# A fused two-block kernel: a new table of engine times for its side work, and key low parts of both attentions on 128 rows

## The chip, the cores and the metric

One core of one Trainium2 chip. The time is the device time of one execution in microseconds (us), the median of repeated runs; the profile is one execution taken apart. Engines: PE (TensorE, matmuls), ACT (ScalarE), DVE (VectorE), POOL (GpSimd) and SP (SyncE, which only starts transfers). Each engine works through its own queue in order and waits for the others by semaphores.

## The reference, cut to what matters

The input `x` has 512 tokens of 1024 features. The first block is a short convolution branch, a gated delta rule with 8 heads of 128 features in chunks of 64 tokens, and a feed-forward net with a convolution. The second block has a pooling mixer, a top-k attention `dsa` and a forgetting attention `fox` with 6 heads of 64 features each, an output projection and a last norm.

```python
# delta rule, per chunk: a triangular system, then a scan over chunks
L = where(strict, einsum('bnhid,bnhjd->bnhij', k_beta, k) * decay, 0.0)
sol = triangular_solve(eye + L, rhs, left_side=True, lower=True)
def step(state, inp):
    v_new = u_c - einsum('bhcd,bhde->bhce', w_c, state)
    o = einsum('bhcd,bhde->bhce', q_c, state) + einsum('bhij,bhje->bhie', A_c, v_new)
    state = state * exp(gl)[..., None] + einsum('bhcd,bhce->bhde', k_c, v_new)
    return state, o
# forgetting attention, F = cumsum(log f):
s = einsum('bqhd,bkhd->bhqk', q[:, s0:e], k[:, :e]) * sm_scale
s = s + F[:, :, s0:e, None] - F[:, :, None, :e]
# dsa: the same product, masked to the keys that a top-k over indexer scores selects
```

## The kernel before, in words

**The main stream.** All activations stand with features on partitions and the 512 tokens along the row. Every projection is cut into tiles of 128 output features (`tiles`, L304 to L348). `run` (L1544) does one tile: for each 128 input features three matmuls of 512 columns, high weight times high activation, high times low, low times high (L1582 to L1586), because each 32-bit value is split into a rounded high part and a low part. I call these the main matmuls. The class `Weights` (L195) loads a tile's weights (`w_raw`, three buffers) by SP's queue, ACT copies the high part (`w_hi`) and POOL or DVE subtracts to give the low part (`w_lo`).

**The side work.** Everything else is written as generators: `head` (L634) and `subst` (L837) for the delta rule, `attend` (L1352) for attention, `ev_keys` (L1238) and its like for what follows each tile. Every six main matmuls `tick` (L370) resumes the generators, and each emits its next few instructions into the engines' queues. A generator is skipped while what it emitted last isn't finished by a guessed clock: `Clock.add` (L76) holds a table of costs per engine and operation and keeps the time at which each engine and each tile is done. So that table decides behind which main matmul a side instruction stands, and in which order DVE, POOL and ACT do theirs. A guess that is too early makes an engine wait in its queue; one that is too late leaves the result unused.

**The delta rule.** For each pair of heads, `subst(p)` inverts triangular blocks in 30 steps of two instructions, on POOL for p = 0 and 2 and on DVE for p = 1 and 3; its matrix `sub_l` comes from DRAM and goes back to DRAM (`dr`) by SP's queue, and a scratch tile is `sub_t`. `head` computes `k` against `k` and `q` with high and low parts `kqh` and `kql` (the low ones made on POOL), then, with the inverse, scans four groups of 128 tokens (L770 to L789): each link is a matmul, then DVE (`r`, or the state `St`) or ACT (`w`), then the next matmul.

**The attentions.** For each pair of heads `ev_queries` makes `q[i]` with the high part of head i on its own 64 rows and its low part on the other 64. `ev_keys` makes `k[0]` and `k[1]`, the high part of each head on all 128 rows, and one tile `k[2]` with the low parts, head 0 on rows 0 to 63 and head 1 on rows 64 to 127. `attend` takes one head and 128 queries at a time, 48 units in all, 12 for each width of 128, 256, 384 and 512 keys. A unit has two matmuls for the scores: `q[i]` against `k[i]` over 128 rows (L1378), and its own 64 rows against those of `k[2]` (L1379). Then DVE adds the mask and takes the maximum, ACT exponentiates, PE transposes and multiplies by the values.

**Memory.** The second block's slots are 29 tiles `slot_c` of 128x512 in the pool `p3`, beside the tiles `fin` of the output (L1661 to L1664).

In the trace, slots are named by their kind (`slot_f`, `slot_x`, `slot_r`, `slot_t` in the first block, `slot_c` in the second); `GT` and `hsm` hold the delta rule's small factors, `cm` constants, `tiny` small columns. Nearly all instructions have the line L142, that of the helper through which they pass, so groups are told apart by their tiles.

Of the kernel before, what the change touches and what calls it, by code (L numbers as in the profile page):

```python
# [11 lines left out]
OP = mybir.AluOpType  # L12
# [41 lines left out]
class Clock:  # L54
# [4 lines left out]
    def __init__(self):  # L59
        self.t = {k: 0.0 for k in ("pe", "act", "v", "p", "dma")}  # L60
        self.end, self.bus = 0.0, {}
        self.wrote, self.read = {}, {}

    @property
    def pe(self):
# [10 lines left out]
    def add(self, kind, method, args, kw):  # L76
        aps = [(k, v) for k, v in [(None, v) for v in args] + list(kw.items())
               if hasattr(v, "tensor") and hasattr(v, "shape")]
        if "out" in kw:
            out = kw["out"]  # L80
        else:
            out = aps.pop(0)[1]
        outs = [out] + [v for k, v in aps if k == "accum_out"]
        ins = [v for k, v in aps if k not in ("out", "accum_out")]
        n = 1
        for v in (kw["in_"] if method == "max" else out).shape[1:]:
            n *= v
        lag = 100
        if method == "dma":
            c = 525  # L90
        elif kind == "pe":
            if method == "transpose":
                c = 109
            elif kw["rhs"].dtype == R32:
                c = max(0.42 * n, 107)
            else:
                c = max(1.68 * n, 1.68 * kw["lhsT"].shape[-1])
            lag = 250
        elif kind == "act":
            c = 70 + 0.88 * n + (180 if isinstance(kw.get("scale"), bass.AP) else 0)  # L100
        elif kind == "v":
            c = 70 + (0.52 if method in ("tensor_scalar", "tensor_copy", "memset") else 1.04) * n
        elif kind == "p":
            c = 145 + (1.2 if method == "memset" else 2.13) * n
            if kw.get("op") == OP.pow:
                c = 950
        s = self.t[kind]
        if not (kind == "pe" and kw.get("start") is False):
            for v in outs:
                k = self.key(v)  # L110
                s = max(s, self.read.get(k, 0), self.wrote.get(k, 0) if kind != "pe" else 0)
        for v in ins:
            s = max(s, self.wrote.get(self.key(v), 0))
        e = self.t[kind] = s + c
        for v in ins:
            k = self.key(v)
            self.read[k] = max(self.read.get(k, 0), e)
        if method == "dma":
            self.bus[kind] = max(self.bus.get(kind, 0), e) + 4 * out.shape[0] * n / 340
            e = self.bus[kind] + 1800  # L120
        e += lag
        for v in outs:
            self.wrote[self.key(v)] = e
        self.end = max(self.end, e)


class Engine:
# [124 lines left out]
def build(tc, A, out):  # L252
# [29 lines left out]
    def slots(pool, kind, n):  # L282
        return [(pool, f"slot_{kind}{i}") for i in range(n)]
# [118 lines left out]
    def need(n, keep=None):  # L402
        while len(FS.free) < n + (reserve[0] if keep is None else keep):
            yield
# [833 lines left out]
    def ev_keys(ps, n, j):  # L1238

        yield from wait_r2()  # L1240
        yield from need(1)
        t = FS.get()
        vtt(t, ps, rrow, OP.mult)
        MB.put(ps)
        yield
        yield from need(3)
        k = [FR.get() for _ in range(3)]
        for i in range(2):
            for o in (64 * i, 64 - 64 * i):
                act(k[i][o:o + 64], t[64 * i:64 * i + 64])  # L1250
        yield
        for i in range(2):
            rows_ = slice(64 * i, 64 * i + 64)
            PL.tensor_tensor(out=k[2][rows_], in0=t[rows_], in1=k[i][rows_].bitcast(F32), op=OP.subtract)
        FS.put(t)
        B2[n, j] = k
        if n == "dk":
            return
        while "F" not in B2:
            yield  # L1260
        yield from need(2)
# [90 lines left out]
    def attend():  # L1352
        while units:
            u = next_unit()
            if u is None:
                yield
                continue
            units.remove(u)
            m, j, qt, i = u
            w = (qt + 1) * 128  # L1360
            tok = slice(qt * 128, qt * 128 + 128)
            if (m, j) not in done:
                obank[m, j] = SB.get()
                done[m, j] = 0
                spawn(finish(m, j))
            P = FS.get()
            if m == "f":
                mask = FS.get()
                act(mask[:, :w], B2["fF", j][i][:, :w], AF.Identity, bias=B2["F"][:, qt, 2 * j + i:2 * j + i + 1])
                ptt(mask[:, w - 128:w], mask[:, w - 128:w], cmask, OP.add)  # L1370
                yield 1000
                while len(SB.free) < 2:
                    yield
            else:
                mask = B2["sel", qt] if qt else amask[:, 384:]
            b = SB.get()
            q, k, half_ = B2[m + "q", j][i], B2[m + "k", j], slice(64 * i, 64 * i + 64)
            PE.matmul(b[:, :w], lhsT=q[:, tok], rhs=k[i][:, :w], start=True, stop=False)  # L1378
            PE.matmul(b[:, :w], lhsT=q[half_, tok], rhs=k[2][half_, :w], start=False, stop=True)  # L1379
            mx, nm = tcol()[:, 0:1], tcol()[:, 0:1]  # L1380
            V.tensor_tensor_reduce(out=P[:, :w], in0=b[:, :w], in1=mask[:, :w], scale=1.0, scalar=-3e38, op0=OP.add,
                                   op1=OP.max, accum_out=mx)
            SB.put(b)
            if m == "f":
                FS.put(mask)
            V.tensor_scalar(out=nm, in0=mx, scalar1=-1.0, scalar2=None, op0=OP.mult)
            yield
# [226 lines left out]
    for i, (kind, key, ids) in enumerate(tiles):  # L1614
# [29 lines left out]
        if kind == "down" and key == 7:  # L1644
            await_(lambda: len(FS.free) == 12, "second phase")
            for j in range(NF):
                RS.put(*act_[j])
            RS.free = [t for t in RS.free if t in BASE]
            P2.close()
            P3 = ctx.enter_context(ExitStack())  # L1650
            p3 = P3.enter_context(tc.tile_pool(name="p3", bufs=1))
            m2 = p3.tile([128, 2, 512], F32, name="m2")
            amask, cmask = m2[:, 0], m2[:, 1, 384:]
            pw = p3.tile([128, 2, 128], F32, name="pw")
            pinv = p3.tile([128, 2, 17], F32, name="pinv")
            misc = p3.tile([128, 56], F32, name="misc")
            top8 = p3.tile([128, 4, 8], F32, name="top8")
            asum = {m: p3.tile([128, 3, 4, 2], F32, name=f"asum{m}") for m in "fd"}
            arec = {m: p3.tile([128, 3, 4, 2], F32, name=f"arec{m}") for m in "fd"}
            spawn(load_consts())  # L1660
            FS = Slots(slots(p3, "c", 29))  # L1661
            FR = Slots(FS.free, R32)
            last = [[p3.tile([128, n, 256], F32, name=f"fin{s}{g}") for g, n in enumerate((3, 3, 2))]
                    for s in range(2)]  # L1664
            reserve[0] = 4
            for q in (1, 2, 3):
                spawn(scores(q))
            spawn(score_cleanup())
            for _ in range(NATT):
                spawn(attend())  # L1670
        if kind == ORDER2[-1][0] and key == ORDER2[-1][1]:
            for j in range(8):
                RS.put(*h2g[j])
# [89 lines left out]
```

## Time and profile before

| | |
|---|---|
| median of 3 runs | 1352.42 us (1351.46 to 1353.33) |
| the profiled execution: its own time | 1349.59 us |
| its span, first to last instruction | 1347.8 us |
| PE busy | 1296.9 us (96%), 6388 matmuls |
| DVE, POOL, ACT busy | 777.1, 698.7, 591.2 us (58, 52, 44%) |
| share of the chain that ended last | PE 80%, DVE 9%, POOL 3% |
| granted TensorE clock, mean | 0.990 of full |

How to read it: the profiled execution was 2.8 us faster than the median of the runs. Matmuls overlap, so the busy time of one is longer than its share; the distance from one start to the next is what a matmul costs. An idle time in brackets behind an instruction names what released it.

### The profile page before, as it was taken

Reading aid. Unit: us, or ns where it says so; the run is one execution under the profiler, and the core shown is the slowest. Engines: PE = TensorE matmul, PEld = TensorE weight load, DVE = VectorE, ACT = ScalarE, POOL = GpSimd, SP = SyncE. Lnnn points to the kernel's source line nnn. Section 1 sums busy time; section 2 is a strip of 40 time slices with the busy share of each in tenths; the row PEclk is TensorE's granted clock in tenths of the full one; section 3 lists DMA queues with packets and bytes.
Section 4 is the critical chain, followed back from the end, with each engine's and each line's share of the span. In section 5 each row is a group of like instructions: output and inputs, shape, how many; then the busy total and the mean of one; then the engine's idle time right before and its main releaser. Section 6 shows DMA issues by size and latency. Waiting matters only on the chain.

```text
span 1347.8 us, 17771 instructions
## 1 busy us (share of the span) xinstructions
PE 1296.9 (96%) x6388; PEld 1058.8 (79%) x6388; DVE 777.1 (58%) x1331; ACT 591.2 (44%) x1348; POOL 698.7 (52%) x624
## 2 busy tenths in 40 slices
PE   6899999899999999999999999999999899999996
PEld 4688787778877788888888888888888677787785
DVE  5667869775757541324576666652334387677533
ACT  5355454554563343333344444443333366654431
POOL 5777882338624132225554444454665665545466
PEclk9999999999999999999999999999999899999998
DMA  6224323232233223334333333233333422112131
GB/s 221 96 71 136 92 86 122 63 114 75 54 115 89 92 64 109 94 112 139 94 95 101 101 95 94 94 102 91 98 102 104 124 76 78 60 51 63 48 93 64
DMA packets 59252, 127.06 MB, mean 94 GB/s; under 512 B 13454, under 2 KB 28046, under 8 KB 59164
## 3 DMA queue, kind: packets, MB, share of 16 engines
q1 hardware_dynamic: 59164, 125.93, 30.3%
q8 instruction: 50, 0.82, 0.3%
q14 instruction: 38, 0.31, 0.1%
HBM read 117.49 MB, written 6.84 MB: 92 GB/s over the span
## 4 chain that ended last, share of the span: by engine, by line
PE 80%; DVE 9%; POOL 3%; issue 3%; ACT 2%; DMA 2%; SPq 0%; DVEq 0%; POOLq 0%; ACTq 0%
PE bank L142 80%; DVE slot_f L142 2%; DVE slot_r L142 2%; DMA w_raw<-in_w_in 2%; POOL w_lo L142 1%; DVE slot_c L142 1%; DVE sub_t L142 1%; ACT slot_f L142 1%; DVE w_lo L142 1%; POOL slot_f L142 1%; DVE sub_l L142 1%; DVE tiny L142 0%; DVE fin L142 0%; ACT w_hi L142 0%; POOL tiny L142 0%
## 5 line engine op out<-in xcount | busy, mean ns | idle before, releaser
L142 PE MATMUL bank<-slot_r,w_hi 128*128 128x512 f32 (+1 forms) x1924 | 611.4, 395 | 1.3 <-POOL slot_r L142 1.3
L142 POOL TENSOR_TENSOR w_lo<-w_raw,w_hi 128x512 fp32r<-128x512 f32 x240 | 317.6, 1329 | 421.9 <-ACT w_hi L142 386.4
L142 PEld LDWEIGHTS bank<-slot_r,w_hi 128*128 128x128 f32 x1924 | 353.9, 189 | 72.1 <-issue 1.9
L142 PE MATMUL bank<-slot_r,w_lo 128*128 128x512 f32 (+1 forms) x944 | 368.0, 390 | 0.7 <-POOL w_lo L142 0.7
L142 ACT ACTIVATE w_hi<-w_raw 128x512 fp32r<-128x512 f32 (+1 forms) x408 | 249.2, 623 | 117.8 <-PE bank L142 92.6
L142 DVE TENSOR_TENSOR w_lo<-w_raw,w_hi 128x512 fp32r<-128x512 f32 x164 | 146.1, 899 | 128.2 <-ACT w_hi L142 124.3
L142 PEld LDWEIGHTS bank<-slot_r,w_lo 128*128 128x128 f32 x944 | 177.9, 188 | 38.8 <-POOL w_lo L142 1.1
L142 PE MATMUL bank<-slot_f,w_hi 128*128 128x512 f32 x488 | 163.4, 406 | 11.1 <-ACT slot_f L142 8.2
L142 PEld LDWEIGHTS bank<-slot_f,w_hi 128*128 128x128 f32 x488 | 90.5, 191 | 34.1 <-ACT slot_f L142 9.9
L142 PE MATMUL bank<-slot_x,w_hi 128*128 128x512 f32 x340 | 113.8, 400 | 0.0
L142 DVE SCALAR_TENSOR_TENSOR slot_b<-slot_b,pc,slot_b 128x511 f32<-128x511 f32 x88 | 87.1, 989 | 22.1 <-ACT slot_b L142 20.5
L142 PE MATMUL bank<-slot_t,w_hi 128*128 128x512 f32 x272 | 96.8, 397 | 0.0
L142 PE MATMUL bank<-slot_f,w_lo 128*128 128x512 f32 x212 | 84.2, 397 | 0.6 <-POOL w_lo L142 0.6
L142 PE MATMUL bank<-slot_x,w_lo 128*128 128x512 f32 x204 | 80.3, 394 | 0.0
L142 PEld LDWEIGHTS bank<-slot_x,w_hi 128*128 128x128 f32 x340 | 62.6, 190 | 12.3
L142 PE MATMUL bank<-slot_a,w_hi 128*128 128x512 f32 x224 | 69.0, 389 | 0.0
L142 ACT ACTIVATE slot_c<-bank 128x512 f32<-128x512 f32 (+5 forms) x82 | 34.9, 466 | 76.5 <-PE bank L142 76.4
L142 PEld LDWEIGHTS bank<-slot_c,slot_c 128*128 128x128 f32 x336 | 48.3, 190 | 18.3 <-issue 12.6
L142 PE MATMUL bank<-slot_c,slot_c 128*128 128x64 f32 (+4 forms) x336 | 62.6, 305 | 0.0
L142 ACT ACTIVATE slot_r<-bank 128x128 f32<-128x128 f32 (+4 forms) x92 | 31.8, 353 | 68.0 <-PE bank L142 50.2
L142 DVE TENSOR_TENSOR slot_x<-bank,slot_x 128x512 f32<-128x512 f32 (+1 forms) x19 | 12.6, 664 | 82.2 <-PE bank L142 82.2
L142 ACT ACTIVATE slot_f<-bank 128x128 f32<-128x128 f32 (+3 forms) x106 | 33.4, 333 | 60.5 <-PE bank L142 44.0
(279 smaller groups left out, 1882.8 us busy)
## 6 DMA issues: line engine op xcount, KB each, us to landing
w_raw<-in_w_in SPq DMA_DIRECT2D x103, 512.0 KB, 3.6
w_raw<-in_w_up SPq DMA_DIRECT2D x44, 512.0 KB, 3.5
w_raw<-in_w_down SPq DMA_DIRECT2D x16, 512.0 KB, 3.6
w_raw<-in_w_a SPq DMA_DIRECT2D x8, 512.0 KB, 3.5
w_raw<-in_w_b SPq DMA_DIRECT2D x8, 512.0 KB, 3.5
w_raw<-in_w_o SPq DMA_DIRECT2D x8, 512.0 KB, 3.5
w_raw<-in_w_out SPq DMA_DIRECT2D x8, 512.0 KB, 3.5
w_raw<-in_w_down SPq DMA_DIRECT2D x8, 384.0 KB, 3.1
```

The lines of the kernel that those rows point to most:

```text
L142: return f(*args, **kw)
```

## The change

First, the table of `Clock.add` is rewritten: delays of 145, 145, 95 and 210 ns from the end of an instruction on ACT, DVE, POOL and PE until another engine may use its result; new costs per operation; 100 ns on PE where the shape of its tile changes; 110 ns for a weight operand that was just made; and DVE and POOL instructions that read the same memory port follow each other. It adds no instruction; it moves side work among main matmuls and in every queue. Second, `ev_keys` makes one low tile per head, on all 128 rows, and `attend` multiplies all 128 rows of `q[i]` by it; the 64 rows with the query's low part then add a product of two low parts. Third, the second block's slots become 37, in a pool of their own, and the output's tiles are taken after it is closed, at the output tile 6.

```diff
@@ Clock.add
-        lag = 100
+        lag = {"act": 145, "v": 145, "p": 95, "pe": 210}.get(kind, 0)
...
+            if whole != self.whole:
+                c += 100
+                s += 100
...
+        if port:
+            for a, b in reversed(self.port["v" if kind == "p" else "p"]):
+                if a <= s < b:
+                    s = b
...
@@ ev_keys
-        yield from need(3)
-        k = [FR.get() for _ in range(3)]
+        yield from need(4)
+        k = [FR.get() for _ in range(4)]
...
             rows_ = slice(64 * i, 64 * i + 64)
-            PL.tensor_tensor(out=k[2][rows_], in0=t[rows_], in1=k[i][rows_].bitcast(F32), op=OP.subtract)
+            for o in (64 * i, 64 - 64 * i):
+                PL.tensor_tensor(out=k[2 + i][o:o + 64], in0=t[rows_], in1=k[i][rows_].bitcast(F32), op=OP.subtract)
@@ attend
-            q, k, half_ = B2[m + "q", j][i], B2[m + "k", j], slice(64 * i, 64 * i + 64)
+            q, k = B2[m + "q", j][i], B2[m + "k", j]
             PE.matmul(b[:, :w], lhsT=q[:, tok], rhs=k[i][:, :w], start=True, stop=False)
-            PE.matmul(b[:, :w], lhsT=q[half_, tok], rhs=k[2][half_, :w], start=False, stop=True)
+            PE.matmul(b[:, :w], lhsT=q[:, tok], rhs=k[2 + i][:, :w], start=False, stop=True)
@@ build
-            FS = Slots(slots(p3, "c", 29))
+            P4 = ctx.enter_context(ExitStack())
+            p4 = P4.enter_context(tc.tile_pool(name="p4", bufs=1))
+            FS = Slots(slots(p4, "c", 37))
...
+        if kind == "wout" and key == 6:
+            await_(lambda: len(FS.free) == 37, "attention")
+            P4.close()
...
+            FS = Slots(slots(p5, "d", 4))
+            last = [[p5.tile([128, n, 256], F32, name=f"fin{s}{g}") for g, n in enumerate((3, 3, 2))]
+                    for s in range(2)]
```

**The first units of attention, on PE.** They are those of the forgetting attention's first two heads. The first operand is a key tile (`slot_c5` and `slot_c6` are the high parts of heads 0 and 1), the second the query tile. A row gives the shape of the output, so the 64 rows of the low product don't show in it. Before:

```order
L142 MATMUL bank7_78<-slot_c5_8624,slot_c10_8725 128x128
L142 MATMUL bank7_78<-slot_c7_8626,slot_c10_8725 128x128
L142 MATMUL bank5_76<-slot_c6_8625,slot_c11_8726 128x128
L142 MATMUL bank5_76<-slot_c7_8626,slot_c11_8726 128x128
L142 MATMUL bank3_74<-slot_c5_8624,slot_c10_8725 128x256
L142 MATMUL bank3_74<-slot_c7_8626,slot_c10_8725 128x256
```

And now:

```order
L171 MATMUL bank3_74<-slot_c5_8621,slot_c11_8721 128x128
L171 MATMUL bank3_74<-slot_c7_8623,slot_c11_8721 128x128
L171 MATMUL bank5_76<-slot_c6_8622,slot_c12_8722 128x128
L171 MATMUL bank5_76<-slot_c8_8624,slot_c12_8722 128x128
L171 MATMUL bank7_78<-slot_c5_8621,slot_c11_8721 128x256
L171 MATMUL bank7_78<-slot_c7_8623,slot_c11_8721 128x256
```

The pairs stand as before; the low tile `slot_c7` served both heads, and now each head has its own (`slot_c7`, `slot_c8`), so that all 48 second matmuls take 128 rows.

**POOL, at the low parts `kql` of the third head.** `sub_t` and `sub_l` are the steps of `subst(0)`, `slot_f_1110` and after the change `slot_f_1109` is a tile of the head before, `slot_f_1373` one of the convolution. Before:

```order
L142 TENSOR_TENSOR sub_t<-sub_l 32x220
L142 TENSOR_TENSOR sub_l<-sub_l,sub_t 32x20x11
L142 TENSOR_TENSOR sub_t<-sub_l 32x228
L142 TENSOR_TENSOR sub_l<-sub_l,sub_t 32x19x12
L142 TENSOR_TENSOR slot_f_1110<-slot_f_1110,slot_f_1263 128x512
L142 TENSOR_TENSOR sub_t<-sub_l 32x234
L142 TENSOR_TENSOR sub_l<-sub_l,sub_t 32x18x13
L142 TENSOR_TENSOR slot_f_1373<-slot_f_1291,slot_f_1372 128x512
L142 TENSOR_TENSOR tiny<-tiny,half 128x4
L142 TENSOR_TENSOR kql<-slot_x_1162,kqh 128x4x128
L142 TENSOR_TENSOR kql<-slot_f_1216,kqh 128x4x128
```

And now:

```order
L171 TENSOR_TENSOR sub_t<-sub_l 32x198
L171 TENSOR_TENSOR sub_l<-sub_l,sub_t 32x22x9
L171 TENSOR_TENSOR slot_f_1109<-slot_f_1109,slot_f_1259 128x512
L171 TENSOR_TENSOR sub_t<-sub_l 32x210
L171 TENSOR_TENSOR sub_l<-sub_l,sub_t 32x21x10
L171 TENSOR_TENSOR kql<-slot_f_1156,kqh 128x4x128
L171 TENSOR_TENSOR kql<-slot_f_1212,kqh 128x4x128
L171 TENSOR_TENSOR slot_f_1373<-slot_f_1287,slot_f_1372 128x512
L171 TENSOR_TENSOR tiny<-tiny,half 128x4
```

Between the decay tile of the head before (the instruction with `cm`, some rows further up) and `kql` stand four pairs of steps, where five stood before, and `slot_f_1373` and `tiny`, which stood ahead of `kql`, now follow it. PE's matmuls of this head come 12 main matmuls earlier too (behind 526, where it was 538).

**DVE, at the first steps of `subst(3)`.** `slot_x_3377` and `slot_r_3426`, after the change `slot_f_3316` and `slot_f_3361`, are the states of the scan of heads 4 and 5; a row with `GT` updates one of them, a row with `hsm` is the next right side `r`. Before:

```order
L142 SCALAR_TENSOR_TENSOR slot_x_3377<-slot_x_3377,GT,bank_74 128x128
L142 TENSOR_TENSOR w_lo<-w_raw,w_hi 128x512
L142 SCALAR_TENSOR_TENSOR slot_r_3751<-slot_r_3751,bank_71 128x512
L142 SCALAR_TENSOR_TENSOR slot_x_3377<-bank_74,hsm,slot_f_2418 128x128
L142 SCALAR_TENSOR_TENSOR slot_r_3426<-slot_r_3426,GT,bank_75 128x128
L142 TENSOR_TENSOR sub_t<-sub_l 32x30
L142 TENSOR_TENSOR sub_l<-sub_l,sub_t 32x30
L142 SCALAR_TENSOR_TENSOR slot_r_3426<-bank_75,hsm,slot_f_2474 128x128
```

And now:

```order
L171 SCALAR_TENSOR_TENSOR slot_f_3361<-bank_77,hsm,slot_f_2453 128x128
L171 TENSOR_TENSOR sub_t<-sub_l 32x30
L171 TENSOR_TENSOR sub_l<-sub_l,sub_t 32x30
L171 TENSOR_TENSOR sub_t<-sub_l 32x58
L171 TENSOR_TENSOR sub_l<-sub_l,sub_t 32x29x2
L171 TENSOR_TENSOR sub_t<-sub_l 32x84
L171 TENSOR_TENSOR sub_l<-sub_l,sub_t 32x28x3
L171 TENSOR_TENSOR w_lo<-w_raw,w_hi 128x512
L171 SCALAR_TENSOR_TENSOR slot_f_3316<-slot_f_3316,GT,bank_78 128x128
L171 SCALAR_TENSOR_TENSOR slot_f_3361<-slot_f_3361,GT,bank_77 128x128
```

The first step of `subst(3)` stood behind the last state update of the scan and now stands ahead of it: in the program it is emitted behind main matmul 1300, where it was 1347. Its last step (1467 before, 1465 now) and the matmuls that use its result (1510 and 1516) stay.

## Rows read from the trace of the kernel before

**Rows 1.** PE's waits over the whole span: us in total, times, longest.

```profile
PE bank L142 <- DVE slot_c L142: 5.4, 2, 4.9
...
PE bank L142 <- POOL kql L142: 2.9, 1, 2.9
...
PE bank L142 <- DVE GT L142: 2.5, 1, 2.5
```

**Rows 2.** Windows: length, busy us of PE, PEld, DVE, ACT, POOL, clock.

```profile
200.00:250.00 50.00, 46.88 (x301) 38.01 (x301) 43.47 (x81) 25.22 (x73) 12.92 (x16) 1.00 0.30 93
1100.00:1300.00 200.00, 199.87 (x1030) 158.42 (x1029) 133.85 (x361) 109.55 (x257) 103.22 (x94) 1.00 0.20 61
```

**Rows 3.** Timeline of PE, units of 384 and 512 keys: start, busy.

```profile
1140.52 1.44 PE L142 MATMUL bank<-slot_c,slot_c 128*128 128x384 f32 x4
1141.88 0.73 PE L142 MATMUL bank<-slot_r,w_hi 128*128 128x512 f32 x2
...
1143.37 0.82 PE L142 MATMUL bank<-slot_c,slot_c 128*128 128x512 f32 x2
1144.12 0.74 PE L142 MATMUL bank<-slot_r,w_hi 128*128 128x512 f32 x2
...
1145.63 0.63 PE L142 MATMUL bank<-slot_r,w_hi 128*128 128x512 f32 x2
...
1146.33 0.62 PE L142 MATMUL bank<-slot_r,w_hi 128*128 128x512 f32 x2
```

**Rows 4.** Timeline of PE, units of 256 keys.

```profile
1213.56 0.59 PE L142 MATMUL bank<-slot_c,slot_c 128*128 128x256 f32 x2
1214.07 0.73 PE L142 MATMUL bank<-slot_r,w_hi 128*128 128x512 f32 x2
```

**Rows 5.** Timeline of PE, main matmuls of 256 columns in the last tile.

```profile
1328.46 0.40 PE L142 MATMUL bank<-slot_r,w_hi 128*128 128x256 f32 x2
...
1328.82 0.40 PE L142 MATMUL bank<-slot_r,w_hi 128*128 128x256 f32 x2
```

**Rows 6.** Timeline of PE, units of 128 keys.

```profile
1253.87 0.98 PE L142 MATMUL bank<-slot_c,slot_c 128*128 128x128 f32 x4
1254.79 0.74 PE L142 MATMUL bank<-slot_r,w_hi 128*128 128x512 f32 x2
```

**Rows 7.** Groups of POOL by form: busy, mean ns, idle before.

```profile
L142 POOL TENSOR_TENSOR slot_c<-slot_c,slot_c 64x512 fp32r<-64x512 f32 x24 | 31.8, 1326 | 1.4
```

**Rows 8.** Timeline of POOL before the third head.

```profile
145.67 1.29 POOL L142 TENSOR_TENSOR slot_f<-slot_f,cm 128x512 f32<-128x512 f32 x1 [0.69 <-issue]
...
157.53 1.28 POOL L142 TENSOR_TENSOR slot_f<-slot_f,slot_f 128x512 fp32r<-128x512 f32 x1
158.78 1.46 POOL L142 TENSOR_TENSOR tiny<-tiny,half 128x4 f32<-128x4 f32 x1
160.22 1.25 POOL L142 TENSOR_TENSOR kql<-slot_x,kqh 128x512 fp32r<-128x512 f32 x1
```

**Rows 9.** Timeline of PE, the third head's products of k.

```profile
162.75 0.39 PE L142 MATMUL bank<-kql,kqh 128*128 128x256 f32 x1 [2.91 <-POOL kql L142]
```

**Rows 10.** Timeline of DVE, the last step of subst(3).

```profile
451.74 0.19 DVE L142 TENSOR_TENSOR sub_l<-sub_l,sub_t 32x30 f32<-32x30 f32 x1
```

**Rows 11.** Timeline of PE, the first use of its result.

```profile
457.83 0.44 PE L142 MATMUL bank<-slot_f,slot_x 32*32 32x32 f32 x16 [2.36 <-DVE slot_f L142]
```

**Rows 12.** Timeline of PE, a link of the first scan (heads 0 and 1).

```profile
263.57 0.49 PE L142 MATMUL bank<-slot_x,slot_r 128*128 128x128 f32 x2 [2.78 <-DVE slot_x L142]
```

**Rows 13.** Timeline of PE, outputs of heads 4 and 5 are transposed.

```profile
425.92 0.30 PE L142 MATMUL bank<-cm,slot_f 128*128 128x128 f32 x1 [1.57 <-DVE slot_f L142]
```

**Rows 14.** Timeline of DVE, the log-sigmoid ahead of the sums F.

```profile
1053.75 5.64 DVE L142 SCALAR_TENSOR_TENSOR slot_c<-slot_c 128x24 f32<-128x24 f32 x8
```

**Rows 15.** Timeline of DVE, the same chain in the first block.

```profile
46.69 1.78 DVE L142 SCALAR_TENSOR_TENSOR slot_r<-slot_r 128x32 f32<-128x32 f32 x8
```

**Rows 16.** Page of the profile: DVE's low parts of weights.

```profile
L142 DVE TENSOR_TENSOR w_lo<-w_raw,w_hi 128x512 fp32r<-128x512 f32 x164 | 146.1, 899 | 128.2 <-ACT w_hi L142 124.3
```

More of the change, by code (lines that the diff above doesn't have):

```diff
@@ L62, in __init__ @@
         self.wrote, self.read = {}, {}
+        self.port, self.whole = {"v": [], "p": []}, True
     @property
@@ L87, in add @@
             n *= v
-        lag = 100
+        s = self.t[kind]
+        lag = {"act": 145, "v": 145, "p": 95, "pe": 210}.get(kind, 0)
         if method == "dma":
@@ L91, in add @@
         elif kind == "pe":
+            m = kw["lhsT"].shape[-1] if "lhsT" in kw else 128
             if method == "transpose":
@@ L94, in add @@
             elif kw["rhs"].dtype == R32:
-                c = max(0.42 * n, 107)
+                c = max(0.417 * n + 13, 112)
             else:
-                c = max(1.68 * n, 1.68 * kw["lhsT"].shape[-1])
-            lag = 250
-        elif kind == "act":
-            c = 70 + 0.88 * n + (180 if isinstance(kw.get("scale"), bass.AP) else 0)
-        elif kind == "v":
-            c = 70 + (0.52 if method in ("tensor_scalar", "tensor_copy", "memset") else 1.04) * n
-        elif kind == "p":
-            c = 145 + (1.2 if method == "memset" else 2.13) * n
+                c = 2 * max(0.833 * n + 4, 0.833 * m + 5)
+            form = "transpose" if method == "transpose" else (kw["lhsT"].shape[0], min(m, 128) // 64)
+            whole = form == "transpose" or form[0] > 64
+            if whole != self.whole:
+                c += 100
+                s += 100
+            self.whole = whole
+        elif kind == "act":
+            c = (46 if self.psum(ins[0]) else 68) + 0.875 * n
+            if isinstance(kw.get("scale"), bass.AP) and not self.psum(ins[0]):
+                c += 98
+            if "accum_out" in kw:
+                c += 93
+        elif kind == "v":
+            c = 75 + (0.52 if method in ("tensor_scalar", "tensor_copy", "memset") else 1.04) * n
+            if method == "scalar_tensor_tensor" and isinstance(kw.get("scalar"), bass.AP):
+                c += 60
+        else:
+            c = 155 + (1.2 if method == "memset" else 2.13) * n
             if kw.get("op") == OP.pow:
-                c = 950
-        s = self.t[kind]
+                c = 990
+        wide = [v for v in ins if not self.psum(v) and v.shape[-1] > 1]
+        port = kind == "p" and method != "memset" or kind == "v" and (
+            len(wide) > 1 or method in ("tensor_scalar", "tensor_copy") and len(wide) == 1)
         if not (kind == "pe" and kw.get("start") is False):
@@ L112, in add @@
         for v in ins:
-            s = max(s, self.wrote.get(self.key(v), 0))
+            s = max(s, self.wrote.get(self.key(v), 0) + (110 if kind == "pe" and v is kw.get("lhsT") else 0))
+        if port:
+            for a, b in reversed(self.port["v" if kind == "p" else "p"]):
+                if a <= s < b:
+                    s = b
+                if b <= s:
+                    break
         e = self.t[kind] = s + c
+        if port:
+            self.port[kind].append((s, e))
         for v in ins:
@@ L124, in add, with psum @@
         self.end = max(self.end, e)
+    @staticmethod
+    def psum(ap):
+        return ap.tensor.name.startswith("bank")
 class Engine:
@@ L1660, in build @@
             spawn(load_consts())
-            FS = Slots(slots(p3, "c", 29))
+            P4 = ctx.enter_context(ExitStack())
+            p4 = P4.enter_context(tc.tile_pool(name="p4", bufs=1))
+            FS = Slots(slots(p4, "c", 37))
             FR = Slots(FS.free, R32)
-            last = [[p3.tile([128, n, 256], F32, name=f"fin{s}{g}") for g, n in enumerate((3, 3, 2))]
-                    for s in range(2)]
             reserve[0] = 4
@@ L1670, in build @@
                 spawn(attend())
+        if kind == "wout" and key == 6:
+            await_(lambda: len(FS.free) == 37, "attention")
+            P4.close()
+            P5 = ctx.enter_context(ExitStack())
+            p5 = P5.enter_context(tc.tile_pool(name="p5", bufs=1))
+            FS = Slots(slots(p5, "d", 4))
+            last = [[p5.tile([128, n, 256], F32, name=f"fin{s}{g}") for g, n in enumerate((3, 3, 2))]
+                    for s in range(2)]
         if kind == ORDER2[-1][0] and key == ORDER2[-1][1]:
```

## The prediction, made before the change was run

> **What bounds the kernel now.** I read the busy times of the page first: PE is busy for 96% of the span, so the time is PE's, and a gain has to be PE time that does nothing or that isn't needed. Then the windows, to see where PE falls short. In the attention stage, from 1100 to 1300 us, PE is busy 199.87 of 200 us and DVE 133.85, POOL 103.22; from 200 to 250 us, where the first delta-rule scans run, PE is busy 46.88 of 50 and DVE 43.47 [rows 2]. So there are two kinds of loss: matmuls that cost more than their columns (they don't show as idle time), and waits that are few and can each be named. Third the waits of PE: the longest single ones, besides the start of the kernel, are 4.9 us for a DVE chain of the forgetting attention, 2.9 us for `kql` and 2.5 us for `GT` [rows 1]. Fourth the timelines at these places, for the step from one matmul's start to the next. A measurement of this kernel can tell about 0.2%, or 2.7 us, from no change.
>
> **The change part by part.** The sum is made against the profiled execution (1349.59 us); it was 2.8 us faster than the median, and I add that at the end.
>
> *Low products on 128 rows.* The change takes 48 changes from a 128-row to a 64-row product and back out of PE's queue, 12 of each width. Three plain matmuls of 512 columns take 1146.33 - 1145.63 = 0.70 us, 0.233 each; three of 256 columns 0.36, 0.12 each [rows 3, 5]. For 384 I take the middle, 0.177. A unit of 512 keys, two matmuls, moves the next start by 0.75 instead of 0.47: 0.28 too much. Two units of 384 keys take 1.36 instead of 0.71: 0.33 each [rows 3]. A unit of 256 takes 0.51 instead of 0.24: 0.27 [rows 4, 5]. Two of 128 take 0.92; at no more than 0.12 a matmul, 0.48 would do: 0.22 each [rows 6]. Twelve of each: 12 x (0.28 + 0.33 + 0.27 + 0.22) = 13.2 us. Besides, the two main matmuls behind such a unit are busy for 0.73 or 0.74 us instead of 0.63 [rows 3, 4, 6]. By my count some 20 stretches of side work end with a unit, which gives 2 us more; behind all 48 it would be 5.3. I take **-15**, with bounds of -13 and -18.5. Nothing else covers this: PE is never idle there.
>
> The price is 12 more POOL instructions of 64x512, since each of six key tiles has four low parts instead of two: 12 x 1.33 = 15.9 us of POOL [rows 7]. Their cover is that PE has work at hand for the whole stage while POOL is busy about half of it [rows 2]; I cost them at nothing except at one place, below. If the cover fails, `attend` waits for its keys by at most 2.65 us per key tile.
>
> *The third head's `kql`.* PE waits 2.91 us [rows 9]. Between the decay tile (ended 146.96) and `kql` (160.22) POOL takes 13.26 us: 1.28 for the convolution's low part (`slot_f_1373`), 1.46 for `tiny`, about another 1.28 for the one other tile, which leaves 9.24 for five pairs of steps, 1.85 each [rows 8]. Now four pairs and one tile stand there: 8.7 us, so `kql` comes 4.6 us earlier. But PE's matmuls come 12 main matmuls earlier too, 12 x 0.233 = 2.8. The wait shrinks by **1.8** (bounds 0 and 2.9: the decay tile may itself be later).
>
> *`subst(3)`.* Its last step ends at 451.93, and PE's first use of the result waits 2.36 us, until 457.83 [rows 10, 11]: the way through DRAM takes the time between, so the end has to come 2.4 us earlier. The first step is emitted 47 main matmuls earlier, 47 x 0.233 = 11 us, the last use stays. I take the whole wait, **-2.4** (bounds 0 and -2.4). What is queued behind it is SP: the weight loads stand behind the transfer of the result, and they come earlier with it.
>
> *The scans.* In the first, PE waits 2.78 us for one link [rows 12], in a stretch where DVE is busy for 43 of 50 us with steps of `subst(1)` between the links. The new order spreads this scan over 156 main matmuls instead of 138 and that of heads 2 and 3 over 90 instead of 78, and `subst(1)` ends 42 later. I take **-2.8** (bounds +2.8, if one such wait only moves, and -5, with smaller ones). The scan of heads 4 and 5 is packed tighter, 72 instead of 84, but the transposes of their outputs now stand 30 main matmuls behind it instead of 12; the 1.57 us there [rows 13] should go: **-1.5** (bounds 0 and -1.6).
>
> *The start.* Instructions move here by a few places in all queues; the wait for `GT` of 2.5 us [rows 1] may go or be doubled. I take **0**, with 2.5 on both sides.
>
> *The chain ahead of `F`.* PE waits 4.9 us for eight tiny DVE instructions that take 5.64 us, 0.70 each [rows 1, 14]; the same chain takes 1.78 us, 0.22 each, in the first block, where POOL did nothing beside it [rows 15]. So a running POOL slows DVE's small work. In the new order four low parts of the first key tile run beside this chain, not two: 2.65 us more of POOL. Half of it on the chain: **+1.3** (bounds 0 and 2.65). The half clock that follows this wait I leave as it is.
>
> The Trainium skill, SBUF — State Buffer, section "SBUF: two separate sides", calls the port pair of DVE and GpSimd an exclusive lock, held for a whole instruction, so that the other engine blocks. By that rule the 12 added instructions could hold DVE for 15.9 us in all, and this chain by the full 2.65. The trace agrees as to the kind: 0.70 instead of 0.22 us [rows 14, 15].
>
> *New waits.* A new order of a thousand side instructions makes waits that the trace of before can't show. By the waits that the old order had, the nearest being the 2.78 and 2.91 us above, I count one of them: **+3** (bounds 0 and 9, three).
>
> The sum: -15 - 1.8 - 2.4 - 2.8 - 1.5 + 0 + 1.3 + 3 = -19.2, so 1330.4 us for an execution like the profiled one, and 1333 us on the scale of the median.
>
> **The rivals.**
>
> *Only the low products pay.* Every gain of the new order is made good by a new wait: -15 + 1.3, so 1338.7 us. For it: a link waits for whatever stands ahead of it in a queue, and everything moved. Against: the two shifts at `kql` and `subst(3)` are larger than what they need.
>
> *The attention stage gives half of it back.* With PE's part 15 us shorter, 185 us hold 134 us of DVE work, at most 150 if every added POOL instruction holds DVE up for all its length, 81%. If half of the 15 turns into waits for masks, maxima and exponentials, 1333 + 7.5 = 1340.5, and about 1343 if a gain of the order fails too. Against: PE showed no wait at all there with DVE at 67%.
>
> *The 64 rows aren't the cause.* The excess might come from the change between score and main matmuls, whatever their rows; then it stays, and only -4.2 is left: 1348 us. Against: the first matmul of a pair, on 128 rows, isn't set apart from the main ones by anything but its bank. The Trainium skill, TensorEngine Tiling (Array Packing), sections "Theoretical Speedup" and "When to Use Tiling", speaks against this edit: a product over 64 rows can run up to twice as fast, beside another one. No row here shows it: a pair with a 64-row member takes longer than two plain matmuls, not less.
>
> *Slower: the moved scan steps wait behind DVE's long work.* The scans of heads 0 to 5 have six DVE links per head, 36 in all. If the new order puts a low part of weights, 0.9 us [rows 16], ahead of most of them, each costs PE that time. To be slower than before the loss must exceed the 19.2 us and the 2.7 that can be told, so a mean of 0.6 us for every link; at 0.7 it is 25 us, 1358 us. For it: DVE at 43 of 50 us, and the 2.78 us of one link, which are this case [rows 2, 12]. Against: two of the three scans are spread wider, not tighter.
>
> **How the numbers follow.** The forecast (low products and most of the order) has 61%, only the low products 19%, half given back 9%, the wrong cause 3%, slower 5%; 3% are left for a sum of small mishaps that comes out level. The forecast is 1333. The low end is 1322: low products at 18.5 (3.5 more), no new wait (3 more), the start's 2.5 and 2 of the scan's smaller waits. The high end, 1343, takes in the first two rivals and leaves out the last two. Faster than 0.2%: 61 + 19 + 9 + 3 = 92%; slower 5%; same 3%.
>
> **What would show it.** In the changed profile the units of 512 keys should move the next start by about 0.47 us and the group of 64-row matmuls should be gone; PE's wait for `kql` should be about 1 us; the wait at the first 32x32 products of heads 6 and 7 should be gone; the wait ahead of `F` should be 5 to 7 us; POOL's group of 64x512 low parts should have 36 members. The prediction is wrong if PE is idle for more than some 5 us between 1100 and 1300, if units of 512 still take 0.75, or if the scans of heads 0 to 5 show more than 6 us of waits for DVE.

## The result, and the profile after

The changed kernel takes 1334.43 us (median of 4 runs, 1333.82 to 1335.42) against 1352.88 (1351.46 to 1354.08): a ratio of 0.9865, 95% interval 0.9848 to 0.9882, or 18.4 us less. The forecast was 1333, in a range of 1322 to 1343. The profiled execution took 1334.81 us, span 1333.0; that of before had been 3.3 us faster than its median, so the two profiles differ by 14.8 us only.

PE's waits over the whole span, the columns as in [rows 1]:

```profile
PE bank L171 <- DVE slot_c L171: 6.3, 1, 6.3
PE bank L171 <- DVE GT L171: 5.2, 1, 5.2
PE bank L171 <- DVE tiny L171: 4.0, 1, 4.0
PE bank L171 <- POOL w_lo L171: 3.3, 2, 2.6
PE bank L171 <- DVE slot_x L171: 3.1, 2, 2.9
...
PE bank L171 <- POOL kql L171: 0.8, 1, 0.8
```

The wait for `kql` went from 2.9 to 0.8 us; those ahead of `F` (`slot_c`) and for `GT` grew; the one for `tiny`, 1.2 us before, is 4.0. Units of attention in PE's timeline, and a window of the stage:

```profile
1126.70 0.63 PE L171 MATMUL bank<-slot_c,slot_c 128*128 128x256 f32 x4
1127.16 0.62 PE L171 MATMUL bank<-slot_r,w_hi 128*128 128x512 f32 x2
...
1129.92 0.51 PE L171 MATMUL bank<-slot_c,slot_c 128*128 128x384 f32 x2
1130.27 0.38 PE L171 MATMUL bank<-cm,slot_c 128*128 128x128 f32 x2
...
1140.75 0.63 PE L171 MATMUL bank<-slot_c,slot_c 128*128 128x512 f32 x2
1141.21 0.49 PE L171 MATMUL bank<-cm,slot_c 128*128 128x128 f32 x3
```

```profile
1100.00:1290.00 190.00, 189.21 (x1047) 160.98 (x1047) 123.28 (x339) 107.49 (x246) 120.52 (x107) 1.00 0.24 70
```

A unit of 512 keys now moves the next start by 0.46 us (0.75 in [rows 3]), one of 384 by 0.35 (0.68), one of 256 by 0.23 (0.51), and PE has work for 189.21 of 190 us. Added up from start to next start, the 96 score matmuls took 30.6 us before and 16.8 now. POOL pays with 12 instructions more (24 in [rows 7]):

```profile
L171 POOL TENSOR_TENSOR slot_c<-slot_c,slot_c 64x512 fp32r<-64x512 f32 x36 | 47.4, 1318 | 1.9
```

Where it loses time is just ahead of that stage. The log-sigmoid chain on DVE, and what POOL does beside it:

```profile
1046.88 8.02 DVE L171 SCALAR_TENSOR_TENSOR slot_c<-slot_c 128x24 f32<-128x24 f32 x8
```

```profile
1046.77 5.26 POOL L171 TENSOR_TENSOR slot_c<-slot_c,slot_c 64x512 fp32r<-64x512 f32 x4
```

On the mean the eight take 1.00 us each, where they took 0.70 before [rows 14]. Some 25 us later DVE accumulates the indexer's scores, slowly, and PE waits for a bank that DVE reads for the first attention unit, queued behind them (`tiny` is its maximum). What POOL does there isn't the added work but products of the residual (`slot_x`), low parts of weights and masks:

```profile
1071.94 6.44 DVE L171 SCALAR_TENSOR_TENSOR slot_c<-slot_c,misc,slot_c 128x256 f32<-128x256 f32 x6
...
1081.95 0.28 DVE L171 CUSTOM_DVE_ANT_0 slot_c<-bank,slot_c 128x128 f32<-128x128 f32 x1
```

```profile
1072.60 3.03 POOL L171 TENSOR_TENSOR slot_x<-slot_x,slot_t 128x512 f32<-128x512 f32 x2
```

```profile
1075.01 0.56 PE L171 MATMUL bank<-slot_c,slot_c 128*128 128x128 f32 x4
...
1082.29 1.25 PE L171 MATMUL bank<-slot_r,slot_r 96*128 96x384 f32 x2 [3.99 <-DVE tiny L171]
1083.34 1.06 PE L171 MATMUL bank<-slot_r,w_hi 128*128 128x512 f32 x2
```

The two main matmuls behind that wait are busy for 1.06 us instead of 0.62: the granted clock is at its lower level (1.2 of 2.4 GHz) for 5.3 us of work. A window of PE alone (length, busy time and matmuls, clock):

```profile
1082.30:1087.60 5.30, 5.30 (x13) 0.50 0.11 46
```

To see where time goes I cut every trace at main matmul 4030 (counted from 0), shortly ahead of `F`. The last column is the place of the first attention unit in PE's queue, as the number of main matmuls ahead of it.

| kernel | start of main matmul 4030 | from there to the end | main matmuls ahead of the first unit |
|---|---|---|---|
| before | 1052.5 | 295.3 | 4130 |
| rows only (old table) | 1054.2 | 286.0 | 4136 |
| rows only, ACT copies | 1054.0 | 281.9 | 4130 |
| table only (64 rows) | 1047.3 | 293.1 | 4124 |
| the change | 1046.8 | 286.3 | 4082 |
| the change, ACT copies | 1047.2 | 275.8 | 4124 |
| the change without the port rule | 1069.9 | 286.2 | 4136 |

The change and its variants with the whole new table have the same instructions on PE up to there, and their executions still reach it between 1044.3 and 1049.0 us. So the first column is known to some 2 us either way; the second is the safer one.

### The profile page after: what moved, and what is told of

Read it like the earlier page. It is cut to its first block, busy times and chain, and to the rows that moved or that the text cites. A ratio compares the mean times of both kernels' runs of the same rounds, so it can differ in the third digit from the quotient of the medians.

```text
span 1333.0 us, 17781 instructions
## 1 busy us (share of the span) xinstructions
PE 1284.2 (96%) x6388; PEld 1059.5 (79%) x6388; DVE 783.2 (59%) x1331; ACT 591.6 (44%) x1348; POOL 717.3 (54%) x636
## 4 chain that ended last, share of the span: by engine, by line
PE 77%; DVE 7%; issue 2%; POOL 2%; ACT 2%; DMA 1%; DVEq 0%; SPq 0%; ACTq 0%; POOLq 0%
PE bank L171 77%; DVE slot_f L171 1%; DVE slot_c L171 1%; DVE w_lo L171 1%; DVE slot_r L171 1%; DVE sub_t L171 1%; DMA w_raw<-in_w_in 1%; ACT slot_c L171 1%; POOL w_lo L171 1%; ACT slot_f L171 1%; DVE sub_l L171 0%; DVE fin L171 0%; POOL slot_c L171 0%; ACT slot_r L171 0%; ACT w_hi L171 0%
## 5 line engine op out<-in xcount | busy, mean ns | idle before, releaser
L171 PE MATMUL bank<-slot_r,w_hi 128*128 128x512 f32 (+1 forms) x2120 | 670.0, 396 | 1.8 <-POOL slot_r L171 1.4
L171 POOL TENSOR_TENSOR w_lo<-w_raw,w_hi 128x512 fp32r<-128x512 f32 x240 | 318.3, 1333 | 408.4 <-ACT w_hi L171 360.8
L171 PEld LDWEIGHTS bank<-slot_r,w_hi 128*128 128x128 f32 x2120 | 389.9, 189 | 77.1 <-POOL slot_r L171 1.8
L171 PE MATMUL bank<-slot_r,w_lo 128*128 128x512 f32 (+1 forms) x1064 | 415.7, 391 | 0.7 <-POOL w_lo L171 0.7
L171 PEld LDWEIGHTS bank<-slot_r,w_lo 128*128 128x128 f32 x1064 | 200.9, 189 | 44.0 <-POOL w_lo L171 1.1
L171 PE MATMUL bank<-slot_x,w_hi 128*128 128x512 f32 x228 | 80.4, 401 | 0.0
L171 PE MATMUL bank<-slot_t,w_hi 128*128 128x512 f32 x204 | 69.8, 397 | 0.0
L171 PE MATMUL bank<-slot_x,w_lo 128*128 128x512 f32 x152 | 59.8, 394 | 0.0
L171 DVE TENSOR_TENSOR slot_b<-bank,rrow 128x512 f32<-128x512 f32 x44 | 30.4, 691 | 43.0 <-PE bank L171 42.9
L171 ACT ACTIVATE slot_r<-bank 128x128 f32<-128x128 f32 (+3 forms) x73 | 26.7, 377 | 58.8 <-PE bank L171 54.9
L171 POOL TENSOR_TENSOR slot_c<-slot_c,slot_c 64x512 fp32r<-64x512 f32 (+1 forms) x38 | 50.0, 1316 | 4.1 <-DVE slot_c L171 2.2
```

The costliest lines, as they stand in the source:

```text
L171: return f(*args, **kw)
```

## The experiments

**Each half alone.** Rows only: the kernel before with the edits of `ev_keys`, `attend` and the pools. Table only: the change with these two functions put back.

```diff
# rows only = before, and
+                PL.tensor_tensor(out=k[2 + i][o:o + 64], in0=t[rows_], in1=k[i][rows_].bitcast(F32), op=OP.subtract)
...
+            PE.matmul(b[:, :w], lhsT=q[:, tok], rhs=k[2 + i][:, :w], start=False, stop=True)
# table only = after, and
+            PL.tensor_tensor(out=k[2][rows_], in0=t[rows_], in1=k[i][rows_].bitcast(F32), op=OP.subtract)
...
+            PE.matmul(b[:, :w], lhsT=q[half_, tok], rhs=k[2][half_, :w], start=False, stop=True)
```

> The kernel before with the low products on 128 rows and the slots they need, and with the old table of engine times. If the changes between 128-row and 64-row products are what they replace, the attention stage loses 13 to 18 us and the wait ahead of F grows by about 1.3: 1336 to 1341 us. If the rows are not the cause and the table made the gain, about 1352 us. The wait for kql stays at 2.9 us and the one for subst(3) at 2.4 in either case.

> The changed kernel with the low products put back on 64 rows (one low tile per pair of heads, two matmuls with 64 rows), the new table and the slots kept. If the 64 rows cost what the trace of before says, 13 to 18 us more than the changed kernel: 1347 to 1352 us, so that the new order alone is worth 0 to 5 us. If the new order made the gain, about 1334 us.

Rows only took 1342.54 us against 1351.58 (ratio 0.9941, 0.9929 to 0.9953), table only 1343.55 (0.9944, 0.9932 to 0.9956). So each half brings 8 to 9 us: the rows less, the table more than expected. PE's waits tell why the rows bring less. Rows only, then table only:

```profile
PE bank L142 <- DVE slot_c L142: 7.7, 2, 7.3
...
PE bank L142 <- DVE tiny L142: 2.9, 1, 2.9
```

```profile
PE bank L171 <- DVE slot_c L171: 3.5, 1, 3.5
```

The wait ahead of `F` is 4.9 with 64 rows and 7.3 with 128 under the old table, 3.5 and 6.3 under the new one: the added low parts cost 2.4 to 2.8 us there under either. The wait for `tiny` comes with them too, and has no row of its own in the table-only run.

**Rows or change of shape.** Both score matmuls on 64 rows; the query's low part times the key's high part is left out.

```diff
-            PE.matmul(b[:, :w], lhsT=q[:, tok], rhs=k[i][:, :w], start=True, stop=False)
-            PE.matmul(b[:, :w], lhsT=q[:, tok], rhs=k[2 + i][:, :w], start=False, stop=True)
+            PE.matmul(b[:, :w], lhsT=q[half_, tok], rhs=k[i][half_, :w], start=True, stop=False)
+            PE.matmul(b[:, :w], lhsT=q[half_, tok], rhs=k[2 + i][half_, :w], start=False, stop=True)
```

> The changed kernel with both score matmuls of a unit on the head's own 64 rows; the product of the query's low part with the key's high part is left out. A unit changes shape once going in and once coming out, as in the kernel before. If the change of shape is the cost, the time is that of the table-only kernel within 3 us, 1346 to 1353. If each 64-row product is slow by itself, by about 0.28 us, another 13 us come on top: 1360 to 1365. If it were worth half the PE time of a 128-row one, it would be under 1334.

1341.07 us (0.9925, 0.9909 to 0.9941): 2.5 below the table-only run, far from 1360, and not under 1334. That time alone settles little, because this kernel keeps the change's POOL work and waits 6.8 us ahead of `F` and 3.7 for `tiny`, where the table-only kernel waits 3.5 and not at all. The rows of the stage say more: PE's group of 512 columns (count, busy time together, mean of one), three units in a row, and one by itself:

```profile
L171 PE MATMUL bank<-slot_c,slot_c 64*128 64x512 f32 x24 | 6.3, 440 | 0.0
```

```profile
1223.72 1.20 PE L171 MATMUL bank<-slot_c,slot_c 64*128 64x512 f32 x6
1224.85 0.73 PE L171 MATMUL bank<-slot_r,w_hi 128*128 128x512 f32 x2
...
1255.42 0.39 PE L171 MATMUL bank<-slot_r,w_lo 128*128 128x512 f32 x1
1255.74 0.73 PE L171 MATMUL bank<-slot_c,slot_c 64*128 64x512 f32 x2
1256.39 0.73 PE L171 MATMUL bank<-slot_r,w_hi 128*128 128x512 f32 x2
```

One unit by itself takes 0.97 us from the start of the main matmul ahead of it to the start of the one behind, where three plain products take 0.69: the way in and out costs 0.28, as for a unit of 512 keys in the kernel before [rows 3]. So it is the change of shape that costs, once per visit. The three units in a row take 1.13 us for six products, less than six plain ones (1.38): the single records show products of the two heads, which stand in turn and use the two halves of the rows, starting 0.01 us apart and running side by side, while products of one head follow each other at 0.23 us, the pace of 128 rows. So the rows aren't slow, and two heads together are faster than on 128 rows. One step of the expectation was wrong: neighbouring units stand together, so the shape changes 24 times each way here, against 48 in the table-only kernel.

**Is it POOL beside DVE?** The low parts of the forgetting attention's keys wait for `F`.

```diff
+        while n == "fk" and "F" not in B2:
+            yield
         for i in range(2):
             rows_ = slice(64 * i, 64 * i + 64)
```

> The changed kernel, but the low parts of the forgetting attention's keys are made only once F is there, so that POOL has none of them beside the log-sigmoid chain. If POOL's running instructions hold DVE's small ones up, the eight scalar_tensor_tensor take 4 us or less instead of 8.0, PE's wait ahead of F falls from 6.3 to 1 to 3.5 us, and with the shorter half-clock stretch behind it 3 to 7 us go: 1327 to 1332. If that chain is late for another reason (its start, ACT's table), the wait stays above 5 us and the time within 2 us of 1334.

1331.43 us (0.9855, 0.9841 to 0.9870): 3.0 below the change by the medians, though the intervals of the ratios overlap. The wait ahead of `F` fell to 1.9 us, and the one for `tiny` rose to 8.0. DVE at both places, and POOL at the second:

```profile
1046.49 3.77 DVE L171 SCALAR_TENSOR_TENSOR slot_c<-slot_c 128x24 f32<-128x24 f32 x8
```

```profile
1069.51 15.46 DVE L171 SCALAR_TENSOR_TENSOR slot_c<-slot_c,misc,slot_c 128x256 f32<-128x256 f32 x10
```

```profile
1067.29 6.45 POOL L171 TENSOR_TENSOR slot_c<-slot_c,slot_c 64x512 fp32r<-64x512 f32 x4
...
1076.83 6.20 POOL L171 TENSOR_TENSOR slot_c<-slot_c,slot_c 64x512 fp32r<-64x512 f32 x4
```

The eight small instructions need 0.47 us each instead of 1.00; the ten score accumulations (of 256 to 512 columns), which now run beside ten POOL instructions, seven of them moved low parts, 1.55 each, about the length of one POOL instruction. The collision moved with POOL's work.

**Other POOL work later.** The eight products of the residual wait for the scores.

```diff
+        while not all(("sc", q) in flags for q in (1, 2, 3)):
+            yield
         for j in range(8):
             yield
             ptt(X1[j], X1[j], t, OP.mult)
```

> The changed kernel, but the eight POOL products that scale the residual for the last norm (slot_x by slot_t) start only once the indexer's scores are done, instead of beside the log-sigmoid chain and the scores. If any running POOL instruction holds DVE up, the wait for tiny (4.0 us) and some of the wait ahead of F (6.3) shrink, by 1.3 us of POOL for each product that stood there: 1328 to 1332 us. If only the low parts of the keys matter, both waits stay within 1 us and the time within 2 us of 1334.

1333.04 us (0.9859, 0.9842 to 0.9875): not to be told from the change. PE's waits did shrink, the longest for `tiny` from 4.0 to 1.2, so that other POOL work holds DVE up as well; the first unit also stands later on PE, behind 4106 main matmuls:

```profile
PE bank L171 <- DVE slot_c L171: 5.3, 1, 5.3
...
PE bank L171 <- DVE tiny L171: 2.1, 2, 1.2
```

**The added instructions taken off POOL.** POOL makes each low part once, ACT copies it.

```diff
-            for o in (64 * i, 64 - 64 * i):
-                PL.tensor_tensor(out=k[2 + i][o:o + 64], in0=t[rows_], in1=k[i][rows_].bitcast(F32), op=OP.subtract)
+            PL.tensor_tensor(out=k[2 + i][rows_], in0=t[rows_], in1=k[i][rows_].bitcast(F32), op=OP.subtract)
         FS.put(t)
+        yield
+        for i in range(2):
+            act(k[2 + i][64 - 64 * i:128 - 64 * i], k[2 + i][64 * i:64 * i + 64].bitcast(F32))
```

> The changed kernel, but POOL makes each low part of the keys once, on the head's own 64 rows (24 instructions in all, as before the change), and ACT copies it to the other 64. If the 12 added POOL instructions are what the attention stage pays with, the wait ahead of F falls to 3.5 us and the one for tiny to under 1.5, as in the table-only kernel, and with the half-clock stretch behind the second one 6 to 9 us go: 1325 to 1329. If ACT's added work makes units wait instead, or the denser order is the cause of the wait for tiny, 1332 to 1336.

1324.63 us (0.9795, 0.9780 to 0.9810), 9.8 less than the change and the best of all. Its wait for `slot_c`, its first units on PE and on DVE, and its window behind `F`, under it that of the change:

```profile
PE bank L171 <- DVE slot_c L171: 3.7, 1, 3.7
```

```profile
1081.56 0.85 PE L171 MATMUL bank<-slot_c,slot_c 128*128 128x128 f32 x6
```

```profile
1083.26 0.28 DVE L171 CUSTOM_DVE_ANT_0 slot_c<-bank,slot_c 128x128 f32<-128x128 f32 x1
```

```profile
1070.00:1090.00 20.00, 19.87 (x96) 16.28 (x95) 15.73 (x27) 16.25 (x39) 17.63 (x14) 1.00 0.43 145
```

```profile
1070.00:1090.00 20.00, 15.29 (x66) 12.34 (x65) 16.36 (x29) 13.11 (x35) 9.77 (x9) 0.83 0.40 132
```

The stage behind main matmul 4030 is 10.5 us shorter: 2.6 ahead of `F`, 4.0 for `tiny`, which is gone, and about 2.6 of the rest the clock (0.50 of full over 5.3 us of PE's work).

The two waits went in different ways. Ahead of `F`, DVE's eight instructions take 5.66 us instead of 8.02, as before the change. But DVE comes to the first unit no earlier than in the change, at 1083.26 us against 1081.95. The wait for `tiny` is gone because the program now has the first unit 42 main matmuls later in PE's queue (1081.56 us against 1075.01), where it had it with 64 rows too. So under the new table the 9.8 us are the price of the added POOL work together with the order that it brings; no run has the one without the other.

**The same under the old table.** The rows-only kernel with ACT's copies.

> The rows-only kernel (old table of engine times) with each low part made once on POOL and copied to the other 64 rows by ACT. If the change of shape is worth 14 to 16 us and POOL's added instructions took 6 of it back, the wait ahead of F returns from 7.3 to about 4.9 us, the one for tiny from 2.9 to under 1.5, and the time is 1334 to 1338 us. If the low products on 128 rows are worth only the 9 us of the rows-only run, 1341 to 1344.

1337.99 us (0.9902, 0.9883 to 0.9921), 14.7 below its runs of before (1352.73) by the medians, 13.3 by the ratio. The first unit stands where it stood before, behind 4130 main matmuls. PE's waits:

```profile
PE bank L142 <- DVE slot_c L142: 4.9, 1, 4.9
...
PE bank L142 <- DVE tiny L142: 1.6, 1, 1.6
```

Both are back near what they were with 64 rows. So the change of shape is worth 13 to 15 us, as forecast, and under the old table POOL's added instructions took 5 to 6 of it back. Under the new table the same step, from the table-only kernel to the one with ACT's copies, is worth 19 us by the medians and 20 by the ratios, 17.3 of it behind main matmul 4030; both wait alike ahead of `F` (3.5 and 3.7) and have the first unit in the same place.

**Low parts on DVE.**

```diff
-                PL.tensor_tensor(out=k[2 + i][o:o + 64], in0=t[rows_], in1=k[i][rows_].bitcast(F32), op=OP.subtract)
+                V.tensor_tensor(out=k[2 + i][o:o + 64], in0=t[rows_], in1=k[i][rows_].bitcast(F32), op=OP.subtract)
```

> The changed kernel with all 24 low parts of 64 rows on DVE instead of POOL, 36 instructions of 64x512 in POOL becoming 12. If the lock between DVE and POOL is the cost, DVE pays about 0.7 us for each of 24 but is held up less: the wait ahead of F falls to about 2 us, and 1326 to 1331. If DVE's own load is what delays the units, the wait for tiny grows and the time is 1335 or more.

1335.01 us (0.9872, 0.9857 to 0.9886), as slow as the change. The wait ahead of `F` is 2.3, but the one for `tiny` stays:

```profile
PE bank L171 <- DVE tiny L171: 4.0, 1, 4.0
```

```profile
1076.96 4.36 DVE L171 TENSOR_TENSOR slot_c<-slot_c,slot_c 64x512 fp32r<-64x512 f32 x4
```

DVE's own queue makes the units late just as well: its 24 instructions take 0.89 us each, and these four stand ahead of the first unit (1083.84), which PE has behind 4106 main matmuls.

**Two combinations.** ACT's copies with the residual's products late, and with the forgetting attention's low parts late.

> The two edits before together. If both lighten POOL at the same two places and add up, 1322 to 1327 us; if the first wait that is taken away only shows the next one, no better than the better of the two alone.

> The kernel with ACT's copies, and the low parts of the forgetting attention's keys made only once F is there. With no POOL instruction of the keys beside the log-sigmoid chain, the wait ahead of F falls from 3.7 to about 1.8 us; the low parts that move are half as many as in the run where POOL made all, so the wait for tiny should stay under 3: 1320 to 1324 us. If they still collide with the scores, 1325 to 1329.

1325.29 (0.9796, 0.9782 to 0.9811) and 1328.70 (0.9826, 0.9807 to 0.9846): nothing beyond the copies alone. In the second the wait ahead of `F` is 2.0, but a new one stands behind it: PE needs a bank of the indexer's scores, which ACT empties only behind four parts of a key tile (64x512, 2.57 us), and these had waited 3.66 us for DVE:

```profile
1086.76 0.80 PE L171 MATMUL bank<-slot_c,slot_c 128*128 128x256 f32 x2 [6.16 <-ACT slot_c L171]
```

**The table without its port rule.** Costs and delays as in the change; DVE and POOL no longer follow each other in the guessed clock.

```diff
-        if port:
+        if False:
             for a, b in reversed(self.port["v" if kind == "p" else "p"]):
```

> The changed kernel with one part of the new table undone: DVE and POOL no longer follow each other in the guessed clock, costs and delays stay. If this rule carries the gain of the new order (about 8 us), 1339 to 1344 us; if costs and delays carry it, 1331 to 1337.

1355.49 us (ratio to before 1.0023, 1.0012 to 1.0033): outside both expectations, 21 us slower than the change. Main matmul 4030 comes 23 us later than in the change, and waits are back all over the first block:

```profile
PE bank L171 <- DVE slot_c L171: 8.3, 1, 8.3
PE bank L171 <- POOL kql L171: 6.0, 3, 2.8
PE bank L171 <- DVE slot_f L171: 5.3, 7, 1.8
PE bank L171 <- POOL w_lo L171: 5.0, 6, 2.6
PE bank L171 <- DVE w_lo L171: 3.7, 4, 1.4
```

With the other new costs, the rule is worth more than the whole gain of the new order; those costs without it are worse than the old table (1342.54 with the same rows). The old costs with the rule were not run.

## Why the prediction was right, and where it wasn't

The time, 1334.43, lies 1.4 us above the forecast and in the middle of the range. The terms did less well than their sum.

- *Low products on 128 rows, -15.* Right in itself: with ACT's copies 13 to 15 us under the old table and 19 to 20 under the new one, and units at the forecast pace. But the step "I cost them at nothing except at one place", for the 12 POOL instructions, was wrong: they cost 5 to 6 us under the old table and, with the order that they bring, 9.8 under the new one. The cover I named was PE's work in the attention stage, and there it held. The price fell due ahead of it, where scores, first keys and first units share DVE's queue. The bound I gave for a failed cover, 2.65 us per key tile, was a price of waiting for keys; what came was DVE held up ahead of `F`, and first units that stand earlier in PE's queue than DVE can serve them.
- *The third head's `kql`, -1.8.* 2.9 to 0.8 us: -2.1.
- *`subst(3)`, -2.4.* Gone: its first products follow the main matmul ahead of them without a wait (it was 2.36 in [rows 11]).
- *The scans, -2.8 and -1.5.* The links' 2.78 us [rows 12] and the outputs' 1.57 [rows 13] have gone; a wait of 2.9 us for `slot_x`, counted below, came at an earlier product of the inverse in the first pair of heads.
- *The start, 0 with 2.5 on both sides.* Main matmul 140 starts at 62.55 instead of 59.70: 2.9 us lost, at the wait for `GT` above all, a little beyond the bound.
- *The chain ahead of `F`, +1.3.* Measured +1.4, but as the sum of two: the new order gave 1.4 (4.9 to 3.5) and the added low parts took 2.8, a little over the upper bound of the step, 2.65, and not half of it.
- *New waits, +3.* 2.6 for `w_lo` and 2.9 for `slot_x` in the first block, 2.8 more for `tiny`, and about 2.6 for the half clock behind it: some 11, above the upper bound of 9.

Up to main matmul 4030 the terms gave -8.5, or -5.5 with the 3 for new waits, and -5.7 was measured. That agreement is in part luck: more was lost at the start and in new waits than the sum allowed, and smaller waits of the kernel before went that it didn't have (1.89, 1.83, 1.05, 1.03 and 0.80 us). Behind it the terms gave -13.7, and -9.0 was measured. On the profiles the sum was thus 4.4 us too hopeful; on the medians the error is 1.4, because I had added 2.8 us for a fast profiled execution of before, and the profiled execution of the change was no fast one but 0.4 above its median. Of the rivals, the one in which attention gives half of the 15 back came closest for its stage, by another way: not by masks and exponentials in the stage, but ahead of it. The rival that the rows aren't the cause has fallen. What the prediction found in no row, 64-row products that gain beside another one, the run with both products on 64 rows shows, where products of the two heads stand next to each other. The slower one didn't come, but the run without the port rule shows how near such a result lay: with another order of the same instructions the kernel ended 2.8 us above the one before, with waits for `kql` and for low parts of weights more than for links of the scans.

## What to carry to other kernels

A product on 64 rows between products on 128 rows costs its change of shape, here 0.2 to 0.4 us per unit; fill the rows, or keep such products together, best with one of each half of the rows next to each other. Before work is added to POOL because it is half idle, look at what DVE does at that moment: most of the price lay in 40 us where PE waited for DVE, once because POOL held DVE's short instructions up and once because units came earlier in PE's queue than DVE could serve them. With a copy on ACT the first wait fell to 3.7 us and the second went. In this kernel a new table of costs gained only with the engines' contention in it.

## What the runs showed of the hardware

DVE instructions with two operands in SBUF were held to the end of the POOL instruction beside them. In the single records one of 128x24 takes 0.18 us when it is free. Of the eight ahead of `F`, two took 1.22 us in the run with late low parts, four 1.13 to 1.22 in the kernel before, and six 1.13 to 1.30 in the change, each ending within 0.05 us of a POOL instruction; that makes the means of 0.47, 0.70 and 1.00, against 0.22 with POOL idle [rows 15]. Ten score accumulations beside ten POOL instructions took 1.55 on the mean, where 0.48 to 0.74 is their time alone, and the POOL low parts among these 1.55 to 1.61 (1.32 on the average of the change). The Trainium skill, SBUF — State Buffer, section "SBUF: two separate sides", has this as an exclusive lock of the two engines' shared port pair; these rows agree, and they show that back-to-back work on both sides takes turns, one of POOL's instructions to one or two of DVE's.

Second, 64-row products on the same half of the rows ran at the pace of 128-row ones (0.23 us for 512 columns), those on the two halves side by side, and a change of shape there and back cost about 0.28 us for a unit of 512 keys. And a wait of 4.0 us cost more than itself: the granted clock was 0.50 in the 5.3 us of work behind it, some 2.6 us, and 0.83 in the 20 us around it, 1.00 in the same stretch of the kernel without that wait.
